# One block more by seven products, late output splits, early weight splits and a shared final scale in a diffusion step

## The chip, the cores and the metric

The kernel runs on one core of a Trainium2 chip. The metric is the device time of one execution in microseconds (us), lower is better. The engines are TensorE (PE in the profile; its weight loads are PEld), VectorE (DVE), ScalarE (ACT), GpSimd (POOL) and SyncE (SP, which here only issues DMAs).

## The reference, cut to what matters

One inference step of a backbone of two layers: a mixer (attention), then a SwiGLU feed-forward network (FFN), each with an adaLN shift, scale and gate, and a final RMS norm. The same weights serve 128 prompt tokens and 512 latent tokens, 640 columns in all, of width 1024.

```python
D_MODEL = 1024; SEQ = 128; DEC_SEQ = 512; DEPTH = 2
D_FF = -(-8 * D_MODEL // (3 * 256)) * 256          # 2816

def rms_norm(x, g):
    y = x * lax.rsqrt(jnp.mean(x * x, axis=-1, keepdims=True) + RMS_EPS)
    return y * g

def swiglu(h, w_in, w_out):
    gate, up = jnp.split(h @ w_in, 2, axis=-1)
    return (jax.nn.silu(gate) * up) @ w_out

# layer 0: 8 heads of latent attention (MLA) beside 8 neighbourhood heads, one output projection
out = jnp.concatenate([a_mla.reshape(b, L, -1), a_na.reshape(b, L, -1)], axis=-1) @ w_out
# layer 1: grouped-query attention; after each mixer: x + gate * swiglu(modulate(rms_norm(x)))
```

## The kernel before, in words

**Layout and precision.** Everything is kept transposed: channels on the 128 partitions, the 640 tokens along the row, worked in two halves of 320 (HALF, HT = 320). The residual stream is eight tiles `xr` of 128x640. An fp32 operand is split into a rounded high part and a low remainder: ScalarE copies to the high part, VectorE (or GpSimd) subtracts to get the low one. A product of two such operands is three matmuls (high x high, high x low, low x high), written by `mm3`, L64. A weight block of 128x1024 is loaded by SP into a `raw` tile and split by `unit` (L173 ACT, L174 DVE).

**Layer 0 mixer.** The latent-attention heads run one after the other. `mts_0` to `mts_4` are the transposed probabilities of a head (L390 ACT high, L391 DVE low), `mo` their product with the values, `oM` the outputs of the heads in pairs, `oN` those of the neighbourhood heads. `rsplit` (L461 ACT, L462 DVE) splits an output into `oMs` and `oNs`, the operands of the output projection `mixer_out` (L1049). `after(inst, fn)` ties the place of an operation in an engine's order to an earlier instruction. `mixer_out` takes its weights from `unit` under the names `oaw0` to `oaw7`. Between its blocks `beside` issues parts of the modulation of layer 1: a load `wm` of 512 KB and two dot products `junk` of 128x1024 on VectorE each (L1630).

**FFN.** The first matrix has 22 blocks `fb` of gate and up rows. `FEW` (L1123) says for each layer how many leading blocks go by plain products (96 matmuls of 128x320 each: 2 matrices x 8 channel blocks x 3 x 2 halves); the others go by a Strassen-Winograd scheme of seven half-size products (84 matmuls: 7 x 4 x 3), prepared by `seven` (L1169) from the two raw halves `wu` and `wg`: four splits `wX`, `wW`, `wY`, `wZ` and four sums `s` on VectorE. A plain block loads its two halves as `wgu` units. `split` (L1364) takes its target from one of two pools in turn, counted by `turn[0]`, which `wout` (L1534) goes on counting: by its parity the second matrix's weight tiles `wo` come from the pool shared with the other loads or from one of their own with a single raw buffer, so the number of earlier splits decides which `wo` load waits for which earlier tile. Hidden blocks are spilled (`sp`) and read back (`hr`) by DMAs on SP's queue. The last block's result passes `up` and `g` on VectorE, which TensorE needs before it adds the last product, `fg<-h01E,wW`. Layer 1's second matrix also goes by seven products (`ffn_out_seven`, L1188).

**The end.** The squares of the final stream are summed by channel block in `fn1acc` (L207 ACT square, L208 DVE add); a matmul with ones sums over the partitions; ACT makes 1/sqrt by ln and exp (`rstd` for the first half, c = 0, `end` for the second, c = 1). `final` (L1894) multiplies each half block by the norm's weight and this factor, on VectorE except blocks 6 and 7 of the second half, which ACT weighs and GpSimd multiplies (L1898), and stores each half block with one DMA of 160 KB, even blocks from ACT's queue, odd ones from SP's.

**What sets the order.** The order on each engine comes from a scheduler that goes by the order of the code, the ties of `after`, the buffers and its own estimates. Each engine then takes its instructions in that order, the issue of DMAs included.

Of the kernel before, what the change touches and what calls it, by code (L numbers as in the profile page):

```python
# [14 lines left out]
ALU = mybir.AluOpType  # L15
# [36 lines left out]
def body(ctx, tc, xT, vecs, crow, wm0, wm0g1, wm0g, wm1, wA, wNV, wNA, wMK, wMV, wOA, wGQ, wGK, wGV, wOC,  # L52
# [96 lines left out]
    def vcol(i):  # L149
        return vec[:, i:i + 1]  # L150
# [44 lines left out]
    class Norm:  # L195
# [20 lines left out]
            S.activation(self.rs[:, c0:c1], self.rs[:, c0:c1], AF.Exp, scale=-0.5)  # L216
            return self.rs

        def end(self, sq, parts):

            pss = bank(f"{self.name}pe")
            PE.matmul(pss[:, :HT], ones, self.acc[:, HT:T], start=True, stop=True)
            for a0, a1 in parts:
                PE.matmul(pss[:, a0:a1], ones, sq[:, a0:a1], start=False, stop=True, skip_group_check=True)
            ln = tp.tile([P, HT], F32, tag="u", bufs=7, name=f"{self.name}ln")
            S.activation(ln, pss[:, :HT], AF.Ln, bias=eps, scale=1.0 / self.n)
            rs = bank(f"{self.name}re")[:, :HT]
            S.activation(rs, ln, AF.Exp, scale=-0.5)
            S.activation(self.rs[:, HT:T], ln, AF.Exp, scale=-0.5)  # L229
            return rs  # L230
# [774 lines left out]
    for h in range(8):  # L1005
        p, r = divmod(h, 2)
        if r == 0:
            oM.append(cp.tile([P, T], F32, tag="om", bufs=4, name=f"oM{p}"))
            pfirst, psecond = prompt_pair([mv[5][:, 2 * p + i, :] for i in range(2)], oM[p], cp, f"mpp{p}",
                                         bank)  # L1010
        pts = []
        sc = mla_scores(h, pts)
        qh, ql = mqs[h]
        pieces = named("s", sc)
        pieces["sp"] = pfirst(r, lambda pss, qh=qh, ql=ql, ks=k_tiles(r, p): mm3(pss, qh[:, NS:T], ql[:, NS:T], ks[0][1], ks[1][1], True, True))
        if h == 0:
            pieces.update({f"b{i}": lambda i=i: mv_late(i) for i in BESIDE})
        if h < 7:
            pieces.update(named("q", mla_q(h + 1)))
            if r == 1:  # L1020
                pieces.update(k_pieces(p + 1, qbank))
        sequence(MLA_ORDER[r], {**pieces, **late, **{k: v for k, v in tail.items() if k not in ("v3", "v4")}})
        late = {"w" + k[1]: tail[k] for k in ("v3", "v4") if k in tail}

        def out_m(ps, h=h, p=p, r=r):
            half_sum(((oM[p][64 * r:64 * r + 64, 0:NS], 0, NS),), ps, NS, cp, f"mhs{h}")
        tail = values(h, pts, lambda b, th, tl, h=h: [(mv[b][:, h, :], th), (mv[b][:, h, :], tl)], cp, "m", out_m)
        if r == 1:
            tail.update(psecond)
        if h in (0, 2, 4, 5):  # L1030
            oNs.append(after(exps[h, 3], lambda: rsplit(oN[len(oNs)], f"oNs{len(oNs)}")))
    oMs = [rsplit(oM[p], f"oMs{p}") for p in range(3)]
    sequence("w3 t0 w4 t1 t2 v0 t3 pt v1 t4 v2 v3 v4 pv", {**tail, **late})
    oMs.append(rsplit(oM[3], "oMs3"))
    mkgs(0, 1)
# [84 lines left out]
                box["m"].make(c, nrm.rs, k)  # L1120
        return box, nxt

    FEW = 4, 3  # L1123
    STAY = 3
    FIRST, SECOND = FO_ORDER[:9], FO_ORDER[9:]

# [61 lines left out]
    def ffn_out_seven(x, nxt, opened, ops, spilt, split, close, last):  # L1188
# [143 lines left out]
        e0.p4()  # L1332
        e1.p7(False)
        e1.p4()
        weighed = {}
        for b in ends:
            b.p5(copied=False)
            result(b.n + 4, 1, b.add("u3", b.b5), -1, True)
            result(b.n, 1, b.held["u2"], 1, False)
            if b is e0:  # L1340
                nrm.rstd(0)
            t = weighed[b.n + 4] = tp.tile([P, HT], F32, tag="u", bufs=7, name=f"xw{b.n}")
            S.activation(t, x[b.n + 4][:, HT:T], AF.Copy, scale=vcol(V_NFIN + b.n + 4))
        e0.go(e0.b5, e0.wZ, 1, "c", False)
        result(e0.n, 1, e0.b5, 1, True)
        e1.go(e1.b5, e1.wZ, 1, "c", False)
        sq = tp.tile([P, HT], F32, tag="u", bufs=7, name="fn1sqe")
        parts = []
        for c0, c1, i in HCOND[1]:
            a0, a1 = c0 - HT, c1 - HT  # L1350
            V.scalar_tensor_tensor(x[e1.n][:, c0:c1], e1.b5[:, a0:a1], mods[1][:, G2 + e1.n, i:i + 1], x[e1.n][:, c0:c1],
                                   ALU.mult, ALU.add)
            S.activation(sq[:, a0:a1], x[e1.n][:, c0:c1], AF.Square)
            parts.append((a0, a1))
        root = nrm.end(sq, parts), weighed
        nxt(x, nrm, 0, range(KT), None)
        ph.close()
        return x, lambda: nxt(x, nrm, 1, range(KT), root)

# [310 lines left out]
    def x_again(n):  # L1670
# [222 lines left out]

    def final(x, nrm, c, ks, root):  # L1894
        c0, c1 = HALF[c]
        for k in ks:
            if root and k in root[1]:
                G.tensor_tensor(x[k][:, c0:c1], root[1][k], nrm.rs[:, c0:c1], ALU.mult)  # L1898
            else:
                V.scalar_tensor_tensor(x[k][:, c0:c1], x[k][:, c0:c1], vcol(V_NFIN + k),  # L1900
                                       root[0] if root else nrm.rs[:, c0:c1], ALU.mult, ALU.mult)
            (nc.sync if k % 2 else nc.scalar).dma_start(yT[:, k, c0:c1], x[k][:, c0:c1])
# [160 lines left out]
```

## Time and profile before

| what | us |
|---|---|
| median of three runs | 1493.82 (1493.72 to 1495.14) |
| the profiled execution, its own time | 1495.92 |
| its span in the trace | 1494.1 |
| TensorE busy | 1448.7 (97%) |
| VectorE busy | 1235.9 (83%) |
| ScalarE busy | 785.7 (53%) |
| GpSimd busy | 178.0 (12%) |

The granted TensorE clock is 0.99 throughout. In a row of the timeline the first number is the start, the second the duration, both in us; a bracket at its end is the idle time of the engine just before, with what ended it. A row of the waits has the waiting instruction, what it waited for, the total, the count and the longest. L64 is the line of all matmuls of `mm3`, so the names of the tiles tell them apart. Matmuls are pipelined: the time from one start to the next is what one costs.

### The profile page before, as it was taken

Reading aid. Unit: us, or ns where it says so; the run is one execution under the profiler, and the core shown is the slowest. Engines: PE = TensorE matmul, PEld = TensorE weight load, DVE = VectorE, ACT = ScalarE, POOL = GpSimd, SP = SyncE. Lnnn points to the kernel's source line nnn. Section 1 sums busy time; section 2 is a strip of 40 time slices with the busy share of each in tenths; the row PEclk is TensorE's granted clock in tenths of the full one; section 3 lists DMA queues with packets and bytes.
Section 4 is the critical chain, followed back from the end, with each engine's and each line's share of the span. In section 5 each row is a group of like instructions: output and inputs, shape, how many; then the busy total and the mean of one; then the engine's idle time right before and its main releaser. Section 6 shows DMA issues by size and latency. Waiting matters only on the chain.

```text
span 1494.1 us, 25843 instructions
## 1 busy us (share of the span) xinstructions
PE 1448.7 (97%) x9766; PEld 1392.5 (93%) x9766; DVE 1235.9 (83%) x2378; ACT 785.7 (53%) x1542; POOL 178.0 (12%) x272
## 2 busy tenths in 40 slices
PE   6999999999999999999999999999999999999997
PEld 4989978889899999999999999989899999999996
DVE  5877778877878888955998888888899989989976
ACT  5446677763745555541222656672665565555443
POOL 0046635420000000000000122220100000000000
PEclk9999999999999999999999999999999999999999
DMA  9643341025154554559765301115154555548561
GB/s 372 207 151 123 114 145 44 15 81 188 42 208 167 166 166 166 163 181 345 234 215 189 96 27 36 37 40 193 57 170 171 190 175 190 174 151 294 184 260 71
DMA packets 79636, 231.48 MB, mean 155 GB/s; under 512 B 8856, under 2 KB 13240, under 8 KB 79128
## 3 DMA queue, kind: packets, MB, share of 16 engines
q1 hardware_dynamic: 77152, 225.43, 44.2%
q10 hardware_dynamic: 1944, 3.48, 0.7%
q8 instruction: 76, 1.25, 0.3%
q0 software_dynamic: 416, 0.93, 0.2%
q14 instruction: 48, 0.39, 0.1%
HBM read 193.15 MB, written 36.66 MB: 154 GB/s over the span
## 4 chain that ended last, share of the span: by engine, by line
PE 77%; DVE 10%; ACT 6%; DMA 4%; issue 2%; POOL 0%; DVEq 0%; ACTq 0%; SPq 0%; POOLq 0%
PE fg L64 19%; PE fd L64 9%; PE fgo L64 5%; PE fu L64 4%; PE gq L64 3%; PE fdo L64 3%; PE fo L64 2%; DVE junk L1630 2%; PE gs L64 2%; PE go L64 2%; PE nk L64 2%; PE nq L64 2%; PE fuo L64 1%; PE gt L68 1%; PE mod L64 1%
## 5 line engine op out<-in xcount | busy, mean ns | idle before, releaser
L1630 DVE SCALAR_TENSOR_TENSOR junk<-wm,cb 128x1024 bf16<-128x1024 f32 x88 | 107.3, 1219 | 1.8 <-DMA wm<-in_wm 1.2
L64 PE MATMUL gq<-h10h,wgq 128*128 128x320 f32 x256 | 65.8, 316 | 0.0
L261 POOL TENSOR_SCALAR h10h<-h10t,gs,mods 128x320 fp32r<-128x320 f32 x4 | 3.1, 786 | 438.2 <-DVE h10t L255 435.9
L1370 ACT ACTIVATE wY<-s 128x1024 fp32r<-128x1024 f32 x37 | 39.2, 1060 | 27.7 <-PE fg L64 24.0
L1898 POOL TENSOR_TENSOR xr<-xw,fn1rs 128x320 f32<-128x320 f32 x2 | 1.7, 866 | 416.9 <-ACT fn1rs L229 416.9
L1370 ACT ACTIVATE wZ<-s 128x1024 fp32r<-128x1024 f32 x37 | 39.1, 1057 | 18.8 <-PE fd L64 16.5
L1479 DVE TENSOR_TENSOR sg<-up,sg 128x640 f32<-128x640 f32 x37 | 30.5, 823 | 20.7 <-ACT sg L1478 19.6
L1371 DVE TENSOR_TENSOR wZ<-s,wZ 128x1024 fp32r<-128x1024 f32 x37 | 45.2, 1222 | 2.8 <-ACT wZ L1370 0.2
L64 PEld LDWEIGHTS gq<-h10h,wgq 128*128 128x128 f32 x256 | 44.9, 189 | 0.6
L1371 DVE TENSOR_TENSOR wY<-s,wY 128x1024 fp32r<-128x1024 f32 x37 | 45.1, 1219 | 0.3
L1478 ACT ACTIVATE sg<-fg 128x320 f32<-128x320 f32 x37 | 16.2, 438 | 48.7 <-PE fg L64 48.7
L64 PE MATMUL fg<-h01q,wgu 128*128 128x320 f32 x192 | 40.3, 316 | 0.9 <-ACT h01q L298 0.5
L1500 ACT ACTIVATE p<-fd 128x320 f32<-128x320 f32 x37 | 16.2, 438 | 46.9 <-PE fd L64 46.9
L64 PE MATMUL gq<-h10l,wgq 128*128 128x320 f32 x128 | 39.4, 308 | 0.0
L1835 ACT ACTIVATE gp<-gs,gb,rq 128x640 f32<-128x640 f32 (+1 forms) x40 | 31.8, 796 | 13.2 <-DVE gb L1834 11.8
L64 PE MATMUL fg<-h11q,wX 128*128 128x320 f32 x228 | 36.7, 309 | 0.0
L64 PE MATMUL fu<-h11q,wX 128*128 128x320 f32 x228 | 36.6, 309 | 0.0
L64 PE MATMUL fd<-h11q,wZ 128*128 128x320 f32 x228 | 36.6, 309 | 0.0
L64 PE MATMUL fg<-h11E,wW 128*128 128x320 f32 x228 | 36.5, 309 | 0.0
L64 PE MATMUL fg<-h11N,wZ 128*128 128x320 f32 x228 | 36.5, 309 | 0.0
L64 PE MATMUL fd<-h11D,wY 128*128 128x320 f32 x228 | 36.4, 308 | 0.0
L64 PE MATMUL fg<-h11C,wY 128*128 128x320 f32 x228 | 36.4, 308 | 0.0
(3425 smaller groups left out, 5331.1 us busy)
## 6 DMA issues: line engine op xcount, KB each, us to landing
wm<-in_wm SPq DMA_DIRECT2D x48, 512.0 KB, 4.3
mraw<-in_wm SPq DMA_DIRECT2D x8, 1024.0 KB, 13.2
mraw<-in_wm SPq DMA_DIRECT2D x16, 512.0 KB, 4.0
wmv<-in_wm0g SPq DMA_DIRECT2D x8, 512.0 KB, 4.3
wm<-in_wm0g SPq DMA_DIRECT2D x8, 512.0 KB, 3.5
ruo<-in_wFO SPq DMA_DIRECT2D x8, 512.0 KB, 4.7
rgo<-in_wFO SPq DMA_DIRECT2D x8, 512.0 KB, 5.9
x<-in_xT SPq DMA_DIRECT2D x8, 320.0 KB, 5.4
```

What stands on the lines that cost most here:

```text
L64: cls.last = nc.tensor.matmul(*a, **k)
L68: cls.last = nc.tensor.transpose(*a, **k)
L261: G.tensor_scalar(h[:, c0:c1], t, self.gsl[:, k, 0:1], self.ml[:, self.sh + k, 0:1], ALU.mult, ALU.add)
L1370: S.activation(h, src, AF.Copy)
L1371: V.tensor_tensor(w_, src, f(h), ALU.subtract)
L1478: last = S.activation(sg[:, 0:HT], g[:, :HT], AF.Silu, scale=-1.0)
L1479: V.tensor_tensor(sg, up, sg, ALU.mult)
L1500: S.activation(p5, b5[:, :HT], AF.Copy)
L1630: V.scalar_tensor_tensor(junk, raw, 1.0, cb[:, c, :], ALU.mult, ALU.mult, accum_out=mods[l][:, j0 + i, c:c + 1])
L1835: gexp[h, j] = S.activation(dst, src, AF.Exp, bias=nb, scale=rq[:, j:j + 1], accum_out=ll[:, j:j + 1])
L1898: G.tensor_tensor(x[k][:, c0:c1], root[1][k], nrm.rs[:, c0:c1], ALU.mult)
```

## The change

1. `FEW` becomes 3, 3: block 3 of layer 0 goes by seven products instead of plain ones.
2. The split `oNs3` is tied to the scores of the last head (head 7, piece 2) instead of head 5, and `oMs0` to `oMs2`, which had no tie, to the last piece of its scores.
3. Layer 0's `mixer_out` gets `early=True`: the next block's weight is asked for before the modulation work of `beside` instead of after it.
4. The end: the first half's blocks 2 to 7 are weighed by ACT in place and multiplied on GpSimd, blocks 0 and 1 stay on VectorE; the second half keeps its sharing (6 and 7 on GpSimd). The products go to ring tiles `y`, two half blocks each, stored by one DMA of 320 KB. The square of the last block but one of the second half no longer passes `fn1acc`: it goes into the sum by a matmul of its own.

```diff
--- before.py
+++ after.py
@@ -216,11 +216,11 @@
             S.activation(self.rs[:, c0:c1], self.rs[:, c0:c1], AF.Exp, scale=-0.5)
             return self.rs
 
-        def end(self, sq, parts):
+        def end(self, parts):
 
             pss = bank(f"{self.name}pe")
             PE.matmul(pss[:, :HT], ones, self.acc[:, HT:T], start=True, stop=True)
-            for a0, a1 in parts:
+            for sq, a0, a1 in parts:
                 PE.matmul(pss[:, a0:a1], ones, sq[:, a0:a1], start=False, stop=True, skip_group_check=True)
             ln = tp.tile([P, HT], F32, tag="u", bufs=7, name=f"{self.name}ln")
             S.activation(ln, pss[:, :HT], AF.Ln, bias=eps, scale=1.0 / self.n)
@@ -1027,9 +1027,10 @@
         tail = values(h, pts, lambda b, th, tl, h=h: [(mv[b][:, h, :], th), (mv[b][:, h, :], tl)], cp, "m", out_m)
         if r == 1:
             tail.update(psecond)
-        if h in (0, 2, 4, 5):
+        if h in (0, 2, 4):
             oNs.append(after(exps[h, 3], lambda: rsplit(oN[len(oNs)], f"oNs{len(oNs)}")))
-    oMs = [rsplit(oM[p], f"oMs{p}") for p in range(3)]
+    oNs.append(after(exps[7, 2], lambda: rsplit(oN[3], "oNs3")))
+    oMs = [after(exps[7, 3], lambda: rsplit(oM[p], f"oMs{p}")) for p in range(3)]
     sequence("w3 t0 w4 t1 t2 v0 t3 pt v1 t4 v2 v3 v4 pv", {**tail, **late})
     oMs.append(rsplit(oM[3], "oMs3"))
     mkgs(0, 1)
@@ -1120,7 +1121,7 @@
                 box["m"].make(c, nrm.rs, k)
         return box, nxt
 
-    FEW = 4, 3
+    FEW = 3, 3
     STAY = 3
     FIRST, SECOND = FO_ORDER[:9], FO_ORDER[9:]
 
@@ -1332,28 +1333,33 @@
         e0.p4()
         e1.p7(False)
         e1.p4()
-        weighed = {}
+        def weigh(k, c):
+            c0, c1 = HALF[c]
+            S.activation(x[k][:, c0:c1], x[k][:, c0:c1], AF.Copy, scale=vcol(V_NFIN + k))
+
         for b in ends:
             b.p5(copied=False)
             result(b.n + 4, 1, b.add("u3", b.b5), -1, True)
             result(b.n, 1, b.held["u2"], 1, False)
             if b is e0:
                 nrm.rstd(0)
-            t = weighed[b.n + 4] = tp.tile([P, HT], F32, tag="u", bufs=7, name=f"xw{b.n}")
-            S.activation(t, x[b.n + 4][:, HT:T], AF.Copy, scale=vcol(V_NFIN + b.n + 4))
+                for k in range(2, KT):
+                    weigh(k, 0)
+            weigh(b.n + 4, 1)
         e0.go(e0.b5, e0.wZ, 1, "c", False)
-        result(e0.n, 1, e0.b5, 1, True)
+        result(e0.n, 1, e0.b5, 1, False)
+        sq = [tp.tile([P, HT], F32, tag="u", bufs=7, name=f"fn1sq{i}e") for i in range(2)]
+        S.activation(sq[0], x[e0.n][:, HT:T], AF.Square)
+        parts = [(sq[0], 0, HT)]
         e1.go(e1.b5, e1.wZ, 1, "c", False)
-        sq = tp.tile([P, HT], F32, tag="u", bufs=7, name="fn1sqe")
-        parts = []
         for c0, c1, i in HCOND[1]:
             a0, a1 = c0 - HT, c1 - HT
             V.scalar_tensor_tensor(x[e1.n][:, c0:c1], e1.b5[:, a0:a1], mods[1][:, G2 + e1.n, i:i + 1], x[e1.n][:, c0:c1],
                                    ALU.mult, ALU.add)
-            S.activation(sq[:, a0:a1], x[e1.n][:, c0:c1], AF.Square)
-            parts.append((a0, a1))
-        root = nrm.end(sq, parts), weighed
-        nxt(x, nrm, 0, range(KT), None)
+            S.activation(sq[1][:, a0:a1], x[e1.n][:, c0:c1], AF.Square)
+            parts.append((sq[1], a0, a1))
+        root = nrm.end(parts), (6, 7)
+        nxt(x, nrm, 0, range(KT), (nrm.rs[:, 0:HT], range(2, KT)))
         ph.close()
         return x, lambda: nxt(x, nrm, 1, range(KT), root)
 
@@ -1678,7 +1684,7 @@
     side, before = mod_side([(0, wm0g, G2)] + [(1, wm1[j:j + 8], j) for j in (SH1, SC1, G1, SH2, SC2)],
                             lambda kind, i: int(i > 4 and i % 3 > 0 or i == 21) if kind == "fb" else
                             (0, 1, 1, 1, 2, 2, 2, 2, 3, 3, 3, 3, 3, 2, 2, 2)[i])
-    x, pend = mixer_out(wOA, oMs + oNs, [4, 5, 6, 7, 0, 1, 2, 3], x_again, mods[0], "oa", nxt, op[-1], before(op[1], op[5], (1, 1, 1, 1, 0, 0, 0)))
+    x, pend = mixer_out(wOA, oMs + oNs, [4, 5, 6, 7, 0, 1, 2, 3], x_again, mods[0], "oa", nxt, op[-1], before(op[1], op[5], (1, 1, 1, 1, 0, 0, 0)), True)
     box2, nxt = next_mod("h10", gs[1][0], mods[1], SH1)
     x, pend = ffn(0, x, pend, box["m"], nxt, side, op)
 
@@ -1893,13 +1899,15 @@
 
     def final(x, nrm, c, ks, root):
         c0, c1 = HALF[c]
-        for k in ks:
-            if root and k in root[1]:
-                G.tensor_tensor(x[k][:, c0:c1], root[1][k], nrm.rs[:, c0:c1], ALU.mult)
-            else:
-                V.scalar_tensor_tensor(x[k][:, c0:c1], x[k][:, c0:c1], vcol(V_NFIN + k),
-                                       root[0] if root else nrm.rs[:, c0:c1], ALU.mult, ALU.mult)
-            (nc.sync if k % 2 else nc.scalar).dma_start(yT[:, k, c0:c1], x[k][:, c0:c1])
+        for i, pair_ in enumerate(((0, 1), (2, 3), (6, 7), (4, 5))):
+            t = ring.tile([P, T], F32, tag="hl", name=f"y{c}{i}")
+            for k, at in zip(pair_, HALF):
+                o = t[:, at[0]:at[1]]
+                if k in root[1]:
+                    G.tensor_tensor(o, x[k][:, c0:c1], nrm.rs[:, c0:c1], ALU.mult)
+                else:
+                    V.scalar_tensor_tensor(o, x[k][:, c0:c1], vcol(V_NFIN + k), root[0], ALU.mult, ALU.mult)
+            (nc.sync if i % 2 else nc.scalar).dma_start(yT[:, pair_[0]:pair_[0] + 2, c0:c1], halves(t))
 
     x, pend = ffn(1, x, pend, box["m"], final, lambda pool: lambda kind, i: None, op)
     pend()
```

The first place is VectorE at the close of layer 0's first FFN matrix, where the last two blocks (20 and 21) end. `wm_8` to `wm_10` are loads of the modulation, `junk` their dot products, `wo_0_...` splits of the second matrix's weights, `g_21` what TensorE waits for. Before:

```order
L1431 TENSOR_TENSOR hd_2l<-sg_20_7644,hd_2h 128x640
L1630 SCALAR_TENSOR_TENSOR junk_8129,mods_99<-wm_8_8127,cb 128x1024
L1506 TENSOR_TENSOR up_21_7775<-fu_21_7774,p_21_7777 128x320
L1630 SCALAR_TENSOR_TENSOR junk_8131,mods_99<-wm_8_8127,cb 128x1024
L1508 TENSOR_TENSOR up_21_7775<-fd_21_7773,u_21_7779 128x320
L1547 TENSOR_TENSOR wo_0_2a<-wo_0_2ar,wo_0_2a 128x768
L1547 TENSOR_TENSOR wo_0_03_8025<-wo_0_03r,wo_0_03_8025 128x768
L1510 TENSOR_TENSOR g_21_7780<-fg_21_7772,p_21_7778 128x320
L1479 TENSOR_TENSOR sg_21_7776<-up_21_7775,sg_21_7776 128x640
```

With the change:

```order
L1516 TENSOR_TENSOR g_20_7657<-fg_20_7649,p_20_7655 128x320
L1636 SCALAR_TENSOR_TENSOR junk_8138,mods_99<-wm_8_8136,cb 128x1024
L1636 SCALAR_TENSOR_TENSOR junk_8140,mods_99<-wm_8_8136,cb 128x1024
L1636 SCALAR_TENSOR_TENSOR junk_8196,mods_99<-wm_9_8194,cb 128x1024
L1636 SCALAR_TENSOR_TENSOR junk_8198,mods_99<-wm_9_8194,cb 128x1024
L1485 TENSOR_TENSOR sg_20_7653<-up_20_7652,sg_20_7653 128x640
L1437 TENSOR_TENSOR hd_2l<-sg_20_7653,hd_2h 128x640
L1512 TENSOR_TENSOR up_21_7784<-fu_21_7783,p_21_7786 128x320
L1636 SCALAR_TENSOR_TENSOR junk_8254,mods_99<-wm_10_8252,cb 128x1024
L1514 TENSOR_TENSOR up_21_7784<-fd_21_7782,u_21_7788 128x320
L1636 SCALAR_TENSOR_TENSOR junk_8256,mods_99<-wm_10_8252,cb 128x1024
L1516 TENSOR_TENSOR g_21_7789<-fg_21_7781,p_21_7787 128x320
```

The dots of `wm_9` and `wm_10`, which stood behind `g_21`, now stand ahead of it, and two weight splits have left their place ahead of it. On SP's queue the loads of `wm_8` and `wm_9` now stand ahead of the reading back of `hr_0`, and that of `wm_10` directly ahead of `hr_2`; before, only `wm_8` stood ahead of `hr_2`.

The second place is ScalarE at the last head of layer 0's latent attention, where `mts_0h` of its second half closes the piece. Before:

```order
L461 ACTIVATE oMs2h<-oM_3496 128x640
L390 ACTIVATE mts_2h<-mt_2_4095 128x512
L965 ACTIVATE mp_2_4087,ml_4024<-ms_2_4078,mn_2_4085 128x640
L390 ACTIVATE mts_3h<-mt_3_4120 128x512
L965 ACTIVATE mp_3_4113,ml_4024<-ms_3_4104,mn_3_4111 128x640
L390 ACTIVATE mts_4h<-mt_4_4142 128x512
L426 ACTIVATE mpp3p,mpp3l_4137<-mpp3s_4131,mpp3m_4135 128x128
L390 ACTIVATE mts_0h<-mt_0_4165 128x512
```

With the change:

```order
L965 ACTIVATE mp_2_4083,ml_4020<-ms_2_4074,mn_2_4081 128x640
L461 ACTIVATE oNs3h<-oN_2366 128x640
L390 ACTIVATE mts_3h<-mt_3_4116 128x512
L965 ACTIVATE mp_3_4109,ml_4020<-ms_3_4100,mn_3_4107 128x640
L461 ACTIVATE oMs0h<-oM_2868 128x640
L390 ACTIVATE mts_4h<-mt_4_4138 128x512
L426 ACTIVATE mpp3p,mpp3l_4133<-mpp3s_4127,mpp3m_4131 128x128
L461 ACTIVATE oMs1h<-oM_3141 128x640
L461 ACTIVATE oMs2h<-oM_3496 128x640
L390 ACTIVATE mts_0h<-mt_0_4165 128x512
```

Four splits of head outputs stand here instead of one, two of them directly ahead of the last `mts_0h`.

The third place is ScalarE at the end of the kernel. `xr_4694` and `xr_4732` are blocks 6 and 7, `fn1sq` squares, L1338 the weighing; `y_17475` holds the first half's blocks 6 and 7. Before:

```order
L216 ACTIVATE fn1rs<-fn1rs 128x320
L1343 ACTIVATE xw_17386<-xr_4694,vec 128x320
L1902 DMA out_yT<-xr_4377 128x320
L207 ACTIVATE fn1sq_17404<-xr_4732 128x320
L1343 ACTIVATE xw_17409<-xr_4732,vec 128x320
L1902 DMA out_yT<-xr_4443 128x320
L207 ACTIVATE fn1sq_17425<-xr_4443 128x320
L1353 ACTIVATE fn1sqe<-xr_4516 128x192
L1353 ACTIVATE fn1sqe<-xr_4516 128x128
```

With the change:

```order
L216 ACTIVATE fn1rs<-fn1rs 128x320
L1338 ACTIVATE xr_4694<-xr_4694,vec 128x320
L1910 DMA out_yT<-y_17475 128x2x320
L207 ACTIVATE fn1sq_17418<-xr_4732 128x320
L1910 DMA out_yT<-y_17467 128x2x320
L1338 ACTIVATE xr_4732<-xr_4732,vec 128x320
L1352 ACTIVATE fn1sq0e<-xr_4443 128x320
L1359 ACTIVATE fn1sq1e<-xr_4516 128x192
L1359 ACTIVATE fn1sq1e<-xr_4516 128x128
```

The store of `y_17475`, which has to wait for GpSimd's third and fourth product, now stands ahead of the square of block 7.

## The prediction

> **What bounds the kernel now.** First the page: busy times and the chain that ended last.
>
> ```profile
> PE 1448.7 (97%) x9766; PEld 1392.5 (93%) x9766; DVE 1235.9 (83%) x2378; ACT 785.7 (53%) x1542; POOL 178.0 (12%) x272
> PE 77%; DVE 10%; ACT 6%; DMA 4%; issue 2%; POOL 0%; DVEq 0%; ACTq 0%; SPq 0%; POOLq 0%
> ```
>
> TensorE is busy 97% of the span, so two things save time: fewer matmuls, and the removal of a wait of TensorE. I therefore read TensorE's waits next, in the windows of the edits: 255 to 385 us (last heads and output projection of layer 0) and 380 to 470 us (first FFN blocks).
>
> ```profile
> PE mo L64 <- DVE mts_4l L391: 1.2, 1, 1.2
> PE mo L64 <- DVE mts_0l L391: 0.5, 2, 0.3
> PE oa3a L64 <- DVE oaw L174: 0.5, 1, 0.5
> PE oa4b L64 <- DVE xr L324: 0.3, 1, 0.3
> PE mpp2o L64 <- DVE mpp2ptl L391: 0.3, 1, 0.3
> ...
> PE fu_3a L64 <- DVE wgu L174: 0.9, 1, 0.9
> ```
>
> None is large; all that the edits can free here is some 3.5 us. The chain of waits at the end is the third view.
>
> ```profile
> 1483.41 0.42 DVE xr L1351
> ...
> 1484.29 1.37 PE fn1pe L64 x6
> ```
>
> After the last FFN matmul the time is a serial tail: update, square, sum, factor, six products, stores, in all 10.7 us from 1483.4 to 1494.1.
>
> **Block 3 by seven products: -2.7.** It takes 84 matmuls instead of 96. What one costs, from two neighbouring groups of twelve:
>
> ```profile
> 659.30 1.92 PE L64 MATMUL fg<-h01N,wZ 128*128 128x320 f32 x12
> 661.06 1.92 PE L64 MATMUL fu<-h01q,wX 128*128 128x320 f32 x12
> ```
>
> 1.76 us from start to start. Twelve fewer: -1.76. The block's plain weight units go too, and with them the wait of 0.94 (rows of the timeline of four engines, in order of time but for the last):
>
> ```profile
> 424.57 0.49 DVE L1464 TENSOR_TENSOR sg<-fu_2a,sg 128x320 f32<-128x320 f32 x1 [3.60 <-ACT sg L1462]
> 427.24 1.06 ACT L1370 ACTIVATE wX<-wu_4r 128x1024 fp32r<-128x1024 f32 x1 [2.75 <-DMA wu_4r<-in_wFI]
> 428.34 1.23 DVE L1371 TENSOR_TENSOR wX<-wu_4r,wX 128x1024 fp32r<-128x1024 f32 x1 [3.27 <-ACT wX L1370]
> 431.05 1.34 PE L64 MATMUL fg<-h01q,wgu 128*128 128x320 f32 x8
> 434.76 2.18 PE L64 MATMUL fu_3a<-h01q,wgu 128*128 128x320 f32 x13 [0.94 <-DVE wgu L174]
> 417.30 0.33 SPq L165 DMA_DIRECT2D wgu_31r<-in_wFI  x1
> ```
>
> In exchange VectorE gets one split of 128x1024 more (1.2), a half split and four sums (half the elements, 0.6 each): 4.2 us, less than the 3.60 + 3.27 that it idles just here. The block's second raw half, `wg_3`, is loaded where `wgu_31` was, at 417.30. That is ahead of `wu_4`, on which ScalarE waits until 427.24, so I take `wg_3` as landed by then; its first sum and split (0.6 + 1.06 + 1.2) are done by 431. TensorE begins the block at 431.05 with `wX`, whose load comes earlier, and needs `wY` twelve matmuls later, at 432.8. Cover: about 2 us. If `wg_3` lands only at 431, the stall is 2. I take 0, ends -0.5 and +2. In all -2.7.
>
> **The turned parity at the close of layer 0's first matrix: +1.1.** One more `split` turns the pools of the `wo` tiles. VectorE's order changes as shown: dots of `wm_9` and `wm_10` now precede `g_21`, for which TensorE's last product waits.
>
> ```profile
> 652.53 0.49 DVE L1508 TENSOR_TENSOR up<-fd,u 128x320 f32<-128x320 f32 x1 [1.34 <-PE fd L64]
> 654.22 0.49 DVE L1510 TENSOR_TENSOR g<-fg,p 128x320 f32<-128x320 f32 x1 [1.20 <-PE fg L64]
> 662.48 1.23 DVE L1630 SCALAR_TENSOR_TENSOR junk<-wm,cb 128x1024 bf16<-128x1024 f32 x1
> 663.63 0.49 DVE L1506 TENSOR_TENSOR up<-fu,p 128x320 f32<-128x320 f32 x1
> 667.31 0.48 DVE L1510 TENSOR_TENSOR g<-fg,p 128x320 f32<-128x320 f32 x1
> 667.86 2.03 PE L64 MATMUL fg<-h01E,wW 128*128 128x320 f32 x12
> ...
> wm<-in_wm SPq DMA_DIRECT2D x48, 512.0 KB, 4.3
> DMA to landing us min/median/max: 3.4/4.9/8.3
> ```
>
> (The last row is for `wm` between 600 and 720 us.) `wm_8` can be issued when the split of `wo_0a`, now ordered just ahead of the `up` at 652.53, has freed its raw tile, at about 652.2; `wm_9` behind that of `wo_2a`, ahead of the `g` at 654.22, at about 654. With a landing time L, `wm_8` is there at 652.2 + L; four dots at 1.15 (662.48 to 663.63) follow, then `wm_10` is issued, lands L later, and dot, `up`, dot (1.15 + 0.41 + 1.14) stand ahead of `g_21`: it starts at 659.6 + 2L instead of 667.31. L = 4.3 makes a stall of 0.9, 4.9 one of 2.1, 3.4 none. TensorE has no other work placed there. I take 1.1, ends 0 and 8.9 (L = 8.3). The other displaced `wo` splits have several us until their use; I give them 0, ends -1 and +1.
>
> **Late output splits: -1.3.** The wait of 1.2 arises from VectorE's queue:
>
> ```profile
> 306.60 1.40 DVE L462 TENSOR_TENSOR oMs1l<-oM,oMs1h 128x640 fp32r<-128x640 f32 x1 [0.24 <-ACT oMs1h L461]
> 307.29 1.44 POOL L868 TENSOR_TENSOR mql<-mqt,mqh 128x320 fp32r<-128x320 f32 x1
> 309.25 1.21 DVE L174 TENSOR_TENSOR oaw<-oaw2r,oaw 128x1024 fp32r<-128x1024 f32 x1
> 311.26 0.50 PE L64 MATMUL mo<-mts_4l,mv 128*128 128x512 f32 x1 [1.16 <-DVE mts_4l L391]
> 315.11 0.75 ACT L461 ACTIVATE oMs2h<-oM 128x640 fp32r<-128x640 f32 x1
> ```
>
> With `oMs1l` (1.40) gone from there, and the split of `oaw2` ahead of `mts_3l` instead of behind it, `mts_4l` comes over a microsecond sooner. The waits of 1.2 (`mts_4l`), 0.3 (the longer of the two for `mts_0l`) and 0.3 (`mpp2ptl`) could all go: -1.8. But the fourth transposition of the next half still hangs on scores, probabilities and GpSimd in a row, and these gain only about 0.6; I give back 0.5. What is late next: the four splits stand before the last `mts_0h`, two of them (0.75 each) directly. TensorE's order gives it twelve more matmuls of the output projection ahead of that point (1.76 us), which cover this, and the last operand, `oMs3`, is wanted only some 80 matmuls (12 us) further on. Without that cover it costs 1.5. Ends -1.8 and +1.5. I take -1.3.
>
> **Early weight splits: -0.5.** The wait of `oa3a` for its weight goes (0.5); the load itself keeps its place on SP's queue. The wait of `oa4b` for an update of `xr` (0.3) may go or grow, since a split of 1.21 now stands ahead of it. Ends -0.8 and +0.9.
>
> **The end: +0.25.** ScalarE, GpSimd and SP at the tail (ACT, POOL, SPq):
>
> ```profile
> 1478.90 0.46 ACT L216 ACTIVATE fn1rs<-fn1rs 128x320 f32<-128x320 f32 x1
> 1481.48 0.47 ACT L207 ACTIVATE fn1sq<-xr 128x320 f32<-128x320 f32 x1 [1.66 <-DVE xr L1214]
> 1486.77 2.84 DVE L1900 SCALAR_TENSOR_TENSOR xr<-xr,vec,fn1re 128x320 f32<-128x320 f32 x6 [0.43 <-ACT fn1re L228]
> 1487.20 1.68 POOL L1898 TENSOR_TENSOR xr<-xw,fn1rs 128x320 f32<-128x320 f32 x2 [416.93 <-ACT fn1rs L229]
> SPq L1902 <- POOL xr L1898: 2.1, 1, 2.1
> 1484.93 0.71 PE L64 MATMUL fn1pe<-fn1sqe,ones 128*128 128x192 f32 x4
> 1489.34 0.91 SPq L1902 DMA_DIRECT2D out_yT<-xr  x2
> out_yT<-xr SPq DMA_DIRECT2D x8, 160.0 KB, 1.9
> ```
>
> GpSimd's first four products run from 1479.4 at 0.84 each, to 1482.8. ScalarE's order puts their store ahead of the square of block 7, so that square moves from 1481.48 to about 1483.1; behind it stand the adding on VectorE and there the update L1357. The sum starts at 1484.05 and takes 0.64 + 0.64 + 0.71 (the second is the new matmul pair for the square that skips the adding): 1486.04 instead of 1485.64, +0.4. That a queue is held so is seen on SP (the row of its waits): its store of a GpSimd product waited 2.1, and the stores behind it went out one behind the other until 1490.3 although the first of their products were older. This goes now: -0.35 on the last issue. A store of 320 KB instead of 160 KB is not in the trace; between 1.9 for 160 and 4.3 for 512 lies +1.1, and the same bytes in fewer issues give 0; I take +0.2. Weighing six blocks on ScalarE costs nothing, in idle stretches like the 1.66 here. Ends -0.65 and +3.4 (GpSimd at 1.44 as in the row at 307.29, four times 0.6 more).
>
> The Trainium skill, "PSUM — Partial Sum Buffer", section "Engine vs sequencer instructions", calls the queues of ScalarE, VectorE and GpSimd strict FIFO; no run here shows ScalarE held by a store, and if it were not, the sum would be 0.7 lower.
>
> **The sum.** -2.7 + 1.1 - 1.3 - 0.5 + 0.25 = -3.15 us. The profiled execution took 1495.92 (span 1494.1), 2.1 more than the median of 1493.82; applied to its 1495.92 the sum is 1492.8, on the scale of the median 1490.7. A measurement of this kernel tells 0.2%, 3.0 us, from no change: below 1490.83 is faster, above 1496.81 slower. The forecast lies at that edge.
>
> **Rivals.** *All as meant*: no stall at the close, all waits go: -2.7 - 1.8 - 0.8 - 0.65 = -5.95, 1487.9. For it: each wait is in the rows. Against it: `wm_10` is ordered ahead of `g_21`.
>
> *GpSimd sets the end*: its products take 1.44 as at 307.29, where VectorE ran beside it, and ScalarE stands behind four of them, 0.6 more each: +2.4, 1493.1. Against it: at 1487.20 two took 0.84 each beside six VectorE products at 0.47 each (2.84 / 6), and neither held the other. The Trainium skill, "SBUF — State Buffer", section "Who interferes with whom", says that a VectorE instruction with two SBUF inputs and a GpSimd instruction that reads SBUF exclude each other; the rows at 306.60 and 307.29 agree, those at 1486.77 and 1487.20 do not.
>
> *The dots of `wm` hold TensorE*: landings as long as the longest shown. The stall is 2L - 7.7; it eats the other gains from L = 6.0, and passes 0.2% slower from L = 7.5. With 8.3 it is 8.9, and the time 1498.5. For it: spills and read-backs share the queue. Against it: `wm_10` now goes ahead of `hr_2` to `hr_5`, and the median is 4.3 to 4.9.
>
> **How the numbers follow.** The forecast has 0.42 (its own range 1489.4 to 1492.1; 0.27 of it below 1490.83), all as meant 0.18, GpSimd 0.18 (a third of it, with late landing of the stores or the projection's cover lost too, beyond 1496.81), the dots 0.22 (0.19 beyond). Faster 0.27 + 0.18 = 0.45; slower 0.06 + 0.19 = 0.25; the rest 0.30. The range from 1488.0 to 1496.5 leaves out the longest landings and the edge of the best case.
>
> **What would show it.** Block 3 in the changed trace: `fg<-h01q,wX` starting without a gap at about 431, no row of waits with `fu_3a`. At the close: a wait of `fg<-h01E,wW` on VectorE's `g` of about 1 us, behind a dot that waits for `wm`. In the heads: no wait for `mts_4l` over 0.5. At the end: the square of block 7 behind a store, its start set by GpSimd. I am wrong if that wait is over 4 us, if `wX` of block 3 waits for its load, or if GpSimd's products take well over 0.9.

## The result and the profile after

The changed kernel takes 1492.1 us (median of 22 runs, 1490.04 to 1497.06); 22 runs of the kernel before beside it gave 1494.46 (1491.67 to 1498.65). The ratio is 0.998, 95% interval 0.9973 to 0.9988: 3.0 us less, between 1.8 and 4.0; the two medians differ by 2.4. The total came out near the predicted -3.15. The parts did not: block 3 and the end are worse than forecast, two other parts better. The profiled execution of the changed kernel has a span of 1489.2 (1491.13 with what lies around it), that of the kernel before 1494.1.

The page after, busy times and chain:

```profile
PE 1445.4 (97%) x9756; PEld 1390.0 (93%) x9756; DVE 1238.4 (83%) x2379; ACT 791.9 (53%) x1553; POOL 185.1 (12%) x278
PE 83%; DVE 8%; ACT 5%; issue 2%; DMA 1%; POOL 0%; ACTq 0%; DVEq 0%; POOLq 0%
```

Nothing has moved in the large. TensorE's waits after (what was waited for: us in total, times, longest), from the heads (255 to 383), the first FFN blocks (378 to 468), the stretch 640 to 850, and the end:

```profile
PE mpp2o L64 <- ACT mts_2h L390: 0.7, 1, 0.7
...
PE fg L64 <- ACT p L1504: 2.3, 1, 2.3
...
PE fg L64 <- DVE g L1516: 0.8, 1, 0.8
...
PE fn1pe L64 <- DVE fn1acc L208: 2.2, 1, 2.2
```

The waits for `mts_4l` (1.2), `oa3a` (0.5), `oa4b` (0.3) and `fu_3a` (0.9) are gone. New are 2.3 on ScalarE's `p` in block 3 and 0.8 on `g` at the close; `mpp2o` waits 0.7 for `mts_2h` instead of 0.3 for `mpp2ptl`; the wait for the last sum of squares, 0.9 before, is 2.2. Two more are gone whose rows the prediction did not show, from the kernel before between 640 and 850:

```profile
PE fn0p L64 <- DVE fn0acc L208: 1.4, 1, 1.4
PE fo_6a L64 <- DVE wo L1547: 0.9, 1, 0.9
```

To price the stages I followed the same matmuls of TensorE through both traces: how much earlier or later each starts after, and where this shift changes.

| stage | shift changes by, us | predicted |
|---|---|---|
| up to 215 us, where no edit lies | -1.42 | - |
| last heads, to `oa0b` (late output splits) | -1.43 | -1.3 |
| `oa3a` (early weight splits) | -1.45, then +0.20: -1.25 | -0.5 |
| block 3 | -2.61, then +1.76: -0.85 | -2.7 |
| close, on `g` | +0.77 | +1.1 |
| `fo_6a`, on a split of `wo` | -1.38 | 0 (-1 to +1) |
| `fn0p` | -1.37 | - |
| the end, from the last gated residual | +1.9 | +0.25 |

With small steps this is the -4.9 between the two spans. The +0.20 and the +1.76 are order: two matmuls of `oa4b` now run behind `oa3a`, and block 3's last product now runs inside block 4. The first row and `fn0p` are not the change's. The first lies ahead of all edits, and it is the clock, which was not 0.99 throughout: from 198 to 208 us it was granted at 0.66 before and at 0.83 after. The wait of `fn0p` is 0.2 or absent in all of the runs below, with the edits or without. Without them -2.1 is left, inside the interval of the ratio.

**Block 3.** Rows of four engines after (start, duration; in brackets the idle time before and what ended it):

```profile
409.65 0.33 SPq L1497 DMA_DIRECT2D wg_4r<-in_wFI  x1
413.19 0.33 SPq L165 DMA_DIRECT2D wg_3r<-in_wFI  x1
420.57 0.69 DVE L1180 TENSOR_TENSOR s<-wg_3r 128x512 f32<-128x512 f32 x1 [4.00 <-DMA wg_3r<-in_wFI]
426.95 1.63 PE L64 MATMUL fg<-h01q,wX 128*128 128x320 f32 x10
428.33 1.06 ACT L1376 ACTIVATE wY<-s 128x1024 fp32r<-128x1024 f32 x1 [1.95 <-DVE s L1181]
429.61 1.05 ACT L1376 ACTIVATE wX<-wu_4r 128x1024 fp32r<-128x1024 f32 x1
430.56 1.04 ACT L1376 ACTIVATE wZ<-s 128x1024 fp32r<-128x1024 f32 x1
431.50 0.72 ACT L1436 ACTIVATE hd_0h<-sg 128x640 fp32r<-128x640 f32 x1
432.13 0.42 ACT L1504 ACTIVATE p<-fg 128x320 f32<-128x320 f32 x1
432.61 2.02 PE L64 MATMUL fg<-h01N,wZ 128*128 128x320 f32 x12 [2.26 <-ACT p L1504]
```

`wg_3` landed at 420.57, 6.4 us ahead of the block, and the block starts without a gap. Its first sums were closed at about 428.6, and `p_3`, the copy that frees their bank for `N`, needs 0.42. It ran at 432.13, since ScalarE had three splits of block 4 and the hidden copy of block 2 (`hd_0h`) ahead of it. The landing of `wg_3` enters by way of VectorE: it idled 4.00 until then, and the first of the three splits waited 1.95 for its sums.

**The end.** DVE, ACT, ACTq and POOL after:

```profile
1470.81 0.68 DVE L1215 SCALAR_TENSOR_TENSOR xr<-u3o,gs,xr 128x192 f32<-128x192 f32 x2
...
1472.60 1.23 DVE L1909 SCALAR_TENSOR_TENSOR y<-xr,vec,fn1rs 128x320 f32<-128x320 f32 x1
1472.61 5.69 POOL L1907 TENSOR_TENSOR y<-xr,fn1rs 128x320 f32<-128x320 f32 x6 [409.11 <-ACT fn1rs L216]
1473.76 0.48 DVE L1240 TENSOR_TENSOR u3o<-fdo,u3o 128x320 f32<-128x320 f32 x1
1474.84 1.91 DVE L1215 SCALAR_TENSOR_TENSOR xr<-u3o,gs,xr 128x192 f32<-128x192 f32 x2
1476.64 0.40 ACTq L1910 DMA_DIRECT2D out_yT<-y  x1
1477.09 0.47 ACT L207 ACTIVATE fn1sq<-xr 128x320 f32<-128x320 f32 x1 [4.11 <-DVE xr L1215]
1477.59 1.05 DVE L208 TENSOR_TENSOR fn1acc<-fn1acc,fn1sq 128x320 f32<-128x320 f32 x1 [0.25 <-ACT fn1sq L207]
```

The square of block 7 (1477.09) starts when ScalarE's store has been issued (1476.64), and this waited for GpSimd's third and fourth product: six took 5.69, 0.95 each. Beside them VectorE is slowed as well: the pair of updates at 1470.81 takes 0.68, the same pair at 1474.84 1.91; the add to `fn1acc` 1.05, 0.49 otherwise. The slowed pair is the update of block 7, which the square reads, and it ended only at 1476.75. So of the 4.11 that ScalarE idled, the store accounts for the last 0.3 alone.

### The profile page after: what moved, and what is told of

Its sections match the earlier page's. It is cut to its first block, busy times and chain, and to the rows that moved or that the text cites. A ratio compares the mean times of both kernels' runs of the same rounds, so it can differ in the third digit from the quotient of the medians.

```text
span 1489.2 us, 25813 instructions
## 1 busy us (share of the span) xinstructions
PE 1445.4 (97%) x9756; PEld 1390.0 (93%) x9756; DVE 1238.4 (83%) x2379; ACT 791.9 (53%) x1553; POOL 185.1 (12%) x278
## 3 DMA queue, kind: packets, MB, share of 16 engines
q8 instruction: 76, 1.25, 0.3%
## 4 chain that ended last, share of the span: by engine, by line
PE 83%; DVE 8%; ACT 5%; issue 2%; DMA 1%; POOL 0%; ACTq 0%; DVEq 0%; POOLq 0%
PE fg L64 18%; PE fd L64 9%; PE fgo L64 5%; PE fo L64 5%; PE fu L64 4%; PE gq L64 3%; PE fdo L64 2%; PE gs L64 2%; PE go L64 2%; PE nk L64 2%; PE nq L64 2%; PE fuo L64 1%; PE gt L68 1%; PE mod L64 1%; PE ms L64 1%
## 5 line engine op out<-in xcount | busy, mean ns | idle before, releaser
L1907 POOL TENSOR_TENSOR y<-xr,fn1rs 128x320 f32<-128x320 f32 x8 | 7.4, 949 | 413.4 <-ACT fn1rs L216 409.1
L64 PE MATMUL fg<-h01N,wZ 128*128 128x320 f32 x228 | 36.6, 309 | 2.3 <-ACT p L1504 2.3
L64 PE MATMUL fg<-h01E,wW 128*128 128x320 f32 x228 | 36.6, 310 | 0.8 <-DVE g L1516 0.8
L64 PE MATMUL fg<-h01q,wX 128*128 128x320 f32 x228 | 36.7, 309 | 0.0
L64 PE MATMUL fd<-h01q,wZ 128*128 128x320 f32 x228 | 36.6, 309 | 0.0
L64 PEld LDWEIGHTS fg<-h01N,wZ 128*128 128x128 f32 x228 | 34.2, 188 | 2.5 <-ACT p L1504 2.5
```

Source lines behind the costliest of these rows:

```text
L64: cls.last = nc.tensor.matmul(*a, **k)
L1907: G.tensor_tensor(o, x[k][:, c0:c1], nrm.rs[:, c0:c1], ALU.mult)
```

## The experiments

Twelve kernels ran. Ten had a single time; the kernel before gave 1495.5 beside the first eight (on two chips), 1495.36 and 1496.19 beside the other two. Single times of one kernel differ by several us (see the ranges above), so for these ten the verdict rests on the waits and on the shift of the same matmuls.

### One part alone

```diff
-    FEW = 4, 3
+    FEW = 3, 3
```


> The kernel before with FEW = 3, 3 alone. Read by the shift of the same matmul's start against the kernel before, stage by stage. Theory: all that the changed kernel shows between 430 and 820 us comes from this one line: -1.76 and the wait for wgu_31 gone, +2.3 of a new wait for ScalarE's copy p in block 3 (net -0.65), +0.8 at the close (wait for g), and -2.75 at the waits for wo_6 and fn0acc; nothing before 400 us beyond the chance shifts of the first 210 us. Rival: the new wait of 2.3 comes from the stream being 4 us early there (heads and projection sped up); then block 3 alone gives -2.7 here.

```diff
-        turn = [0]
+        turn = [1 - l]
```


> The kernel before with the counter of splits started at 1 instead of 0 in layer 0, nothing else: block 3 stays plain, the wo tiles change pools. Theory (parity): +0.8 at the close and -2.75 at the waits of fo_6a and fn0p, so -2 in all; first FFN blocks unchanged. Rival: these waits went because the stream before them was earlier; then nothing changes at 712 to 818 us.

```diff
-    ... before(op[1], op[5], (1, 1, 1, 1, 0, 0, 0)))
+    ... before(op[1], op[5], (1, 1, 1, 1, 0, 0, 0)), True)
```


> The kernel before with early = True in layer 0's output projection alone. Theory A: the -1.45 at the start of oa3a belongs to this edit. Rival B, the term as predicted: -0.5 here, the rest of the 1.45 belongs to the late splits. Rest of the kernel unchanged either way.

```diff
-        if h in (0, 2, 4, 5):
+        if h in (0, 2, 4):
...
+    oNs.append(after(exps[7, 2], lambda: rsplit(oN[3], "oNs3")))
+    oMs = [after(exps[7, 3], lambda: rsplit(oM[p], f"oMs{p}")) for p in range(3)]
```


> The kernel before with the late output splits alone. Theory: -1.4 between the start of the last heads and the start of oa0b, as in the changed kernel, and nothing at oa3a. Rival: if the order of the weight splits is what cost at oa3a, up to -1 there too.

The fifth has only the new end, as in the diff of the change.

> The kernel before with the new end alone. Theory: the time from the end of the last FFN matmul to the end of the span grows from 10.7 to 12.7 us as in the changed kernel, +2.0, with the same +1.3 at the start of the last sums. Rival: part of it comes from other edits (the stream's state at the end); then less than +1.

| alone | time, us | TensorE's waits and shifts against the kernel before |
|---|---|---|
| block 3 by seven | 1492.19 | `p` 1.4; block 3 -3.42, +1.77; `g` 1.4; `fo_6a` -1.38 |
| turned parity | 1496.12 | `g` 0.5; `fo_6a` -1.18 |
| early weight splits | 1496.3 | `oa3a` -2.08, then +0.49 and +0.29; `g` 0.3; `fo_6a` still 0.9 |
| late output splits | 1494.03 | heads -1.4; `oa3a` +1.63 (its wait 2.1 instead of 0.5); `g` 0.4; `fo_6a` still 0.9 |
| new end | 1497.34 | `fn1pe` 2.2 instead of 0.9, +1.10; `g` 0.6; `fo_6a` still 0.9 |

What follows. The times of the turned parity and of the early splits are no lower because each lost 1.5 near 880 us, where the clock fell (last section). The wait for `p` in block 3 comes with block 3 by seven and needs no other edit. It is 1.4 here and not 2.3, so block 3 gains 1.65, between the theory's 0.65 and the rival's 2.7. The gain at `fo_6a` is there exactly in the runs with turned parity. The wait on `g` is 0 to 0.6 in the four profiles without it, the kernel before among them, 0.3 on the mean, and 0.3 to 2.1 in the ten with it, the changed kernel and the runs below among them, 1.0 on the mean: the turned parity costs about 0.7. This is a rough size, since the two ranges overlap. The rows of the changed kernel show how, as forecast:

```profile
660.44 1.22 DVE L1636 SCALAR_TENSOR_TENSOR junk<-wm,cb 128x1024 bf16<-128x1024 f32 x1 [0.84 <-DMA wm<-in_wm]
663.13 0.48 DVE L1516 TENSOR_TENSOR g<-fg,p 128x320 f32<-128x320 f32 x1
663.67 2.03 PE L64 MATMUL fg<-h01E,wW 128*128 128x320 f32 x12 [0.81 <-DVE g L1516]
```

Early alone is worth 1.3, the -2.08 less what comes back with the order of the matmuls. The kernel before shows where it lies:

```profile
347.62 0.31 PE L64 MATMUL oa4a<-oNs0l,oaw 128*128 128x320 f32 x1
348.22 0.39 PE L64 MATMUL oa4b<-oNs0h,oaw 128*128 128x320 f32 x1 [0.29 <-DVE xr L324]
348.44 0.31 PE L64 MATMUL oa4b<-oNs0l,oaw 128*128 128x320 f32 x1
349.26 0.41 PE L64 MATMUL oa3a<-oNs0h,oaw 128*128 128x320 f32 x1 [0.51 <-DVE oaw L174]
```

The next matmul starts at 349.51. From 347.62 to there four matmuls take 1.89, and at 0.147 from start to start (1.76 for twelve) they would take 0.59. The two waits cost 1.3, though their idle time is 0.8. Both are gone with the early order.

The two splits of the mixer are no sum. Late alone gives its 1.4 back at `oa3a`, and only with the early order is it kept. The low split of the fourth weight on VectorE, first with late splits alone, then in the changed kernel:

```profile
346.56 1.22 DVE L174 TENSOR_TENSOR oaw<-oaw3r,oaw 128x1024 fp32r<-128x1024 f32 x1
```

```profile
343.09 1.21 DVE L174 TENSOR_TENSOR oaw<-oaw3r,oaw 128x1024 fp32r<-128x1024 f32 x1
```

With late alone the split stands behind two dots more. It came at 347.98 in the kernel before, and the 1.4 by which it is sooner here is about the 1.7 that this run was ahead when it reached the heads; TensorE, 1.4 sooner besides, waits for it longer.

### The end taken apart

On the changed kernel, first with all stores of the first half on SyncE:

```diff
-            (nc.sync if i % 2 else nc.scalar).dma_start(yT[:, ...], halves(t))
+            (nc.sync if i % 2 or c == 0 else nc.scalar).dma_start(yT[:, ...], halves(t))
```


> The changed kernel with all stores of the first half issued from SP, so that no store that waits for GpSimd stands on ScalarE. Theory A (ScalarE held by the store): the square of block 7 is no longer late, the tail falls from 12.7 to about 10.5. Theory B (VectorE and GpSimd hold each other): VectorE's products of the first half still take 0.8 to 1.2 instead of 0.55 and its two updates of block 7 1.9 instead of 0.7, so the sum is only some 0.5 earlier, the tail about 12.2.

Then, besides, with the first half's products on VectorE alone (GpSimd keeps the last two):

```diff
-                for k in range(2, KT):
-                    weigh(k, 0)
...
-        nxt(x, nrm, 0, range(KT), (nrm.rs[:, 0:HT], range(2, KT)))
+        nxt(x, nrm, 0, range(KT), (nrm.rs[:, 0:HT], ()))
```


> The changed kernel with the first half's products all on VectorE as before, stores of the first half from SP; square into the matmul and paired stores kept. Theory A and B alike: no GpSimd work beside VectorE, the tail 10.3 to 10.7. If paired stores of 320 KB land later: above 10.7 although the sums start no later than before.

The measure is the time from the last gated residual (`xr<-fgo,gs,xr`) to the span's end. It is 18.3 to 18.7 in the six profiles with the old end, 19.9 to 21.0 in five with the new (20.4 on the mean and in the changed kernel), 19.4 with the stores moved and 17.7 without GpSimd. So the new end costs 1.9. Moving the stores gives back about half of that. In the expectation's terms the tail falls from 12.7 to 11.6, between theory A (10.5) and theory B (12.2). The square of block 7 comes only 0.3 sooner after the last gated residual (8.0 instead of 8.3, 5.9 in the kernel before), so the store held ScalarE for little. The add to `fn1acc` won more: it now stands ahead of GpSimd's last product and takes 0.53 instead of 1.05, while that product takes 1.10 behind it. The rest stays, because VectorE is still slowed (run with the stores on SyncE, POOL, DVE and ACT):

```profile
1474.41 5.94 POOL L1907 TENSOR_TENSOR y<-xr,fn1rs 128x320 f32<-128x320 f32 x6 [409.03 <-ACT fn1rs L216]
1476.65 1.91 DVE L1215 SCALAR_TENSOR_TENSOR xr<-u3o,gs,xr 128x192 f32<-128x192 f32 x2
1478.48 0.40 DVE L1215 SCALAR_TENSOR_TENSOR xr<-fdo,mods,xr 128x192 f32<-128x192 f32 x1
1478.59 0.47 ACT L207 ACTIVATE fn1sq<-xr 128x320 f32<-128x320 f32 x1 [3.82 <-DVE xr L1215]
1479.09 0.53 DVE L208 TENSOR_TENSOR fn1acc<-fn1acc,fn1sq 128x320 f32<-128x320 f32 x1 [0.21 <-ACT fn1sq L207]
```

Without GpSimd beside them the same instructions take their usual times:

```profile
1478.17 0.55 DVE L1907 SCALAR_TENSOR_TENSOR y<-xr,vec,fn1rs 128x320 f32<-128x320 f32 x1
1479.50 0.68 DVE L1215 SCALAR_TENSOR_TENSOR xr<-u3o,gs,xr 128x192 f32<-128x192 f32 x2
1480.88 0.48 DVE L208 TENSOR_TENSOR fn1acc<-fn1acc,fn1sq 128x320 f32<-128x320 f32 x1
```

Which ones are slowed has a rule in the rows. Those with two tensors in SBUF are (`y<-xr,vec,fn1rs`, `xr<-u3o,gs,xr`, `fn1acc`); those with one of the two in PSUM are not (`u3o<-fdo,u3o` 0.48, `xr<-fdo,mods,xr` 0.40, both while GpSimd runs). That is what the Trainium skill states in "SBUF — State Buffer", section "Who interferes with whom": VectorE and GpSimd share one pair of ports and lock each other out of it. The trace agrees: the pair of updates goes from 0.68 to 1.91, GpSimd's product from 0.84 to 0.95. It also resolves the rows that the prediction held against the rule: in the last stretch VectorE's factor `fn1re` is a PSUM bank, so six products there take 2.84 beside GpSimd as they do alone.

### Block 3: the load, or the queue on ScalarE

Five runs keep the change's order on ScalarE here. In each, 12.0 us pass from the sum that waits for `wg_3` to `fg<-h01N,wZ`, whatever the wait, which goes from 1.3 to 3.1 with the landing. Either the load is late, or too much stands between it and `p_3`. First, block 4's splits behind `p_3`:

```diff
-            wX, wW, wY, wZ = seven(ru, rg, f"{l}_{fb}", fp, split)
+            wX, wW, wY, wZ = after(p1i if l == 0 and fb == few + 1 else None, lambda: seven(ru, rg, f"{l}_{fb}", fp, split))
...
-            S.activation(p1, g[:, :HT], AF.Copy)
+            p1i = S.activation(p1, g[:, :HT], AF.Copy)
```


> The changed kernel with block 4's weight preparation tied behind ScalarE's copy p of block 3. Theory (ScalarE's queue): the wait of 2.3 in block 3 shrinks, to 0 if the copy of the hidden block 2 ahead of it is not late either, to 1.5 or more if that one, which needs VectorE's product of block 2, is what holds it. Rival: the weights of block 4 come late instead and TensorE waits for them by 2 us at the start of block 4.

The wait falls from 2.3 to 1.1, and block 3 is 1.1 shorter; the time was 1488.62. What was left is the hidden copy, so next this went behind `p_3` too:

```diff
             p1i = S.activation(p1, g[:, :HT], AF.Copy)
+            if l == 0 and fb == few:
+                after(p1i, lambda: hidden(few - 1, late))
+                step("fb", few - 1)
```


> Moves the hidden copy of layer 0's block 2 (hd) behind the first copy of block 3 (p_3) on ScalarE, on top of block 4's splits being behind it. Theory (the whole wait of fg<-h01N,wZ in block 3 is ScalarE's queue): in the run with only the splits moved, p_3 started at 430.11, 0.64 after the hidden copy began at 429.47, and TensorE waited 1.13; here p_3 starts as soon as its sums are closed and the wait is under 0.2, so the time is some 1.0 us below that run, about 1487.6. Rival (what is moved comes back at block 4, whose weights and hidden copies now run later): the wait goes but fg<-h01q,wX of block 4 waits 0.8 or more for its weights, and the time stays at 1488.6.

Rows of it, DVE, ACT and PE (the hidden copy is `hd_2h` in this kernel):

```profile
418.68 0.69 DVE L1180 TENSOR_TENSOR s<-wg_3r 128x512 f32<-128x512 f32 x1 [3.15 <-DMA wg_3r<-in_wFI]
427.57 0.44 ACT L1506 ACTIVATE p<-fg 128x320 f32<-128x320 f32 x1 [1.47 <-PE fg L64]
427.91 0.73 ACT L1436 ACTIVATE hd_2h<-sg 128x640 fp32r<-128x640 f32 x1
429.14 1.92 PE L64 MATMUL fg<-h01N,wZ 128*128 128x320 f32 x12
436.17 1.93 PE L64 MATMUL fg<-h01q,wX 128*128 128x320 f32 x12
```

ScalarE now waits for TensorE and not the other way, the wait is gone, and block 4 follows without one (436.17): the rival falls. The time, 1488.89, is not lower: TensorE lost 1.5 again near 872 us, where its granted clock was 0.61 for 4 us; no edit lies there.

Last, the load alone: the changed kernel with `wg_3` ahead of `wg_4` on SyncE's queue.

```diff
-            if fb == few or l and fb % 2:
+            if fb == few and l or l and fb % 2:
```


> The changed kernel with the second weight of layer 0's block 3 (wg_3) in the pool of two buffers, so that its load is issued ahead of block 4's (wg_4), where wg_4's was (409.65), instead of behind it and behind a load of 1024 KB (413.19). In five runs that keep the change's order on ScalarE the wait at fg<-h01N,wZ follows the landing of wg_3: from the split that waits for it to that matmul 12.04 us each time. Theory 1 (block 3's own load is what is late): wg_3 lands by about 414 and the wait is gone, block 3 is 2.3 us shorter than in the changed kernel, the time about 1489. Theory 2 (p_3 is late because block 4's splits stand ahead of it in ScalarE's queue): these now wait for wg_4, issued at about 416 with some 8 us to landing, and the wait stays between 1 and 3 us, though block 3's own weights are ready; the time stays within 1 us of the changed kernel's 1491.

```profile
408.21 0.33 SPq L1497 DMA_DIRECT2D wg_3r<-in_wFI  x1
411.77 0.62 ACT L1177 ACTIVATE wW<-wg_3r 128x512 fp32r<-128x512 f32 x1
422.83 0.64 ACT L1177 ACTIVATE wW<-wg_4r 128x512 fp32r<-128x512 f32 x1 [2.91 <-DMA wg_4r<-in_wFI]
429.30 0.43 ACT L1504 ACTIVATE p<-fg 128x320 f32<-128x320 f32 x1
429.77 2.02 PE L64 MATMUL fg<-h01N,wZ 128*128 128x320 f32 x12 [0.85 <-ACT p L1504]
```

`wg_3` is split at 411.77, 13.8 us ahead of the block, and still TensorE waits 0.85 for `p_3`, now behind splits that wait for `wg_4`. The first theory wanted no wait and is out; the second wanted 1 to 3, and 0.85 is just under it. The 1.4 won here is given back at later waits, and the time, 1491.22, is the changed kernel's. So the stall is the queue on ScalarE; a load only sets how far block 4's splits run late in it.

### Both cures, and the change with the old end

The best version is the changed kernel with `p_3` ahead of block 4's splits and of the hidden copy, and with the first half's end on VectorE and SyncE, by the diffs above.

> The changed kernel with p_3 ahead of the hidden copy and of block 4's splits, and with the first half's final scales on VectorE alone and all its stores on SyncE. Theory (block 3's wait of 2.3 us is ScalarE's queue alone, and the end loses to GpSimd's six products 2.65 us, 20.35 of the end with them against 17.7 without): 1494.5 - 3.0 - 2.3 - 2.65 = 1486.5, ratio to before 0.9947. Rival (gains at block 3 are taken back by later waits for weights): only the end's part stays, 1488.9, ratio 0.9962. Rival (the end's loss was the chance of single profiles): only block 3's part, 1489.2, ratio 0.9965.

It took 1486.33 (five runs, 1484.66 to 1489.02) against 1495.36 (nine), ratio 0.9945, interval 0.9933 to 0.9958: 8.2 us less than the kernel before, and faster than the changed kernel, whose interval it doesn't touch. Both rivals, 0.9962 and 0.9965, lie outside. No wait for `p` or `fn1pe` is left:

```profile
PE fg L64 <- DVE g L1519: 0.3, 1, 0.3
...
PE fn1p L64 <- DVE fn1acc L208: 0.6, 1, 0.6
```

The other has all of the change but its end, that is the first three edits on the kernel before.

> The change without its new end: block 3 by seven, late output splits and early weight splits, with the end of the kernel before. Theory (the new end costs 1.8 us, by the time from the last gated residual to the span's end, 18.5 in five profiles with the old end and 20.35 in three with the new): 1494.5 - 3.0 - 1.8 = 1489.7, ratio to before 0.9968. Rival (the prediction's term of +0.25): 1491.2, ratio 0.9978.

1489.25 (five runs), ratio 0.9961, interval 0.9947 to 0.9975. The theory's 0.9968 is inside, the prediction's 0.9978 just outside: the times of the whole kernel, too, speak for an end that costs more than 0.25.

## Why the prediction was right in sum and wrong in parts

**Block 3 (-2.7; -0.85 in the profile).** The twelve matmuls and the wait for `fu_3a` went as said. The fear was the wrong one: I asked whether `wg_3` lands in time, took a stall of 0 and an end of +2. It landed with 6.4 us to spare, and the wait of 2.3 came from what was queued between it and `p_3` on ScalarE. The step that failed compared VectorE's extra 4.2 us with its idle time and asked nothing of ScalarE. Its order, `p_3` behind three splits of block 4 and a hidden copy (1.06, 1.05, 1.04 and 0.72), was to be had before the run, as VectorE's was for the close.

**The close (+1.1; about +0.7).** Right in place and mechanism, and near in size. The long landings of the rival did not occur; the wait was never over 2.1.

**The other displaced `wo` splits (0; -1.2 to -1.4).** Mis-sized, just beyond the end of -1. The turned pools also move the split of the first part of `wo_6` on VectorE ahead of dots of `wm`, and the wait of 0.9 at `fo_6a`, which I had not looked up, goes with it.

**Late output splits (-1.3; -1.43)** and **early weight splits (-0.5; -1.25).** The first is right in the changed kernel, but only there: alone it is worth nothing. The second was mis-sized, alone too (1.3). I priced it at the idle time of one wait, 0.5; that of `oa4b` goes as well, and both cost TensorE more from start to start than their idle time. On top of the late splits it is worth nearly 3, since with these alone the wait at `oa3a` is 2.1 and eats their gain. I priced two edits to one queue one by one.

**The end (+0.25; +1.9).** The order was right, the square of block 7 stands behind the store; but the step that made this hold the cost was wrong. The store holds the square for 0.3. What is late is the square's own operand, since GpSimd slows VectorE's update of block 7. The rule of the Trainium skill that was weighed there ("PSUM — Partial Sum Buffer", "Engine vs sequencer instructions": strict FIFO) holds for a store's issue too, by these 0.3. GpSimd's product took 0.95 instead of 0.84, and VectorE's instructions beside it up to nearly three times their time, which no term held. The rival *GpSimd sets the end* (+2.4) was the nearer one; I put it at 0.18 on the strength of two rows in which VectorE read PSUM. The last store's gain and the longer landing (320 KB took 2.3 and 2.6 against 1.9 and 1.8 for 160) nearly cancel.

Block 3 and the end came out 3.5 worse, the early splits and `wo` some 2 better, and the close 0.4. That the total was near is luck: misses of both signs met.

## What to carry to other kernels

Price a moved block by every engine's queue up to the instruction that frees its bank, and not by its load alone: a short copy that TensorE waits for belongs ahead of the splits of the next block. An idle GpSimd is no free helper beside a VectorE that works on two SBUF tensors; look at which operands are in PSUM before a row is taken as proof that they don't meet. A wait of TensorE can cost more than its idle time in the list; price it from start to start. Two edits that feed one engine's queue are priced together, since the second may be worth nothing, or everything, through the first.

## What the hardware showed unexpectedly

TensorE's granted clock falls for some 4 us at a time: 0.61 from 871.5 to 875.5 in the run with both moves on ScalarE (1.5 us lost), 0.63 from 433.5 to 438 in the run without GpSimd's six products, there right behind a wait of 3.1; behind the wait of 2.2 at the changed kernel's end it was 0.77, and the last four matmuls of the sum took 1.16 instead of 0.71. Three other runs lose the same 1.5 at the same queries and scores of layer 1 (870 to 883), with no idle time of TensorE over 0.3 in the 10 us before, and of three other waits of some 2 us one was followed by such a stretch (667.6 in the run without the six products, 0.58 from 669 to 673), and two were not (432.6 in the changed kernel, 347.8 with the late output splits alone). The Trainium skill, "TensorE: Matmul & The Clock Gate", section "HAM oscillation — how this bites in real kernels", asks for idle gaps above some 3.4 us; the longest gap ahead of these stretches is the 3.1, so by these rows it is not the whole rule. What sets a stretch off stays open; they are part of why single times differ.
